# Placing attention's groups between projections by the planner's running estimate of TensorE's time

## Chip, cores and metric

The kernel runs on one core of a Trainium2 chip. The metric is the device time of one execution in microseconds (us); less is better. TensorE does the matmuls and transposes, VectorE, ScalarE and POOL (GpSimd) the elementwise work, and SyncE issues most of the DMAs from one queue (SPq in the rows).

## What is computed

One layer of a streaming encoder for 512 prompt tokens and 32 sample tokens (with 512 cached positions), width 1024, all in float32:

```python
h = rmsnorm(x, norm_mix); proj = h @ w_in            # q, k, v | RWKV-7 parts | gates A, B
o = diff_attend(q, k, v, lam, mask)                  # 8 heads, two softmax maps each
    # s = q k^T / 8 ; p = softmax(s) ; pd = p[0] - lam * p[1] ; o = pd @ v
o_da = (rmsnorm(o, da_subln) * (1 - lam_init)) @ w_o_da
o_rw = rwkv7_time_mixing(...) @ w_o_rw               # recurrence per token, group norm, gate
x = x + (sigmoid(gA) * o_da + sigmoid(gB) * o_rw) @ w_out
x = x + convffn(rmsnorm(x, norm_ffn)) ; y = rmsnorm(x, norm_final)
```

For the prompt the attention is causal by chunks of 64 tokens; for the sample it runs over the cache and its own 32 tokens, without a mask.

## The kernel before

**Stages.** The kernel computes the projections of `w_in` together with the recurrence, then attention, then the output projections (`w_orw`, `w_oda`, `w_out`) and the feed-forward part. The change lies in the attention stage, which begins when the recurrence's pools close (about 598 us in the profile) and ends when the first matmul of the `w_oda` projection starts (831 us).

**Projections.** `dense_g` (L229) makes one tile of 128 output columns. Weights and activations are split into high and low parts, so each of 8 steps of the inner dimension takes three matmuls of 128x128 by 272 columns, for each of two halves of the tokens: 16 steps a tile. A step ends at a `yield`. At the start of attention ten tiles of `w_in` are left (the gates; `fillers`, `fill_tile` L904), and eight tiles of the recurrence's output projection follow (`orw_g` L1392, which needs `z` from the recurrence in the split form `mh`, `ml`, loaded by `load_z` L1150, and a buffer `mg`).

**Attention.** `attention` (L1318) runs over 8 heads and four blocks of 128 queries each. One block is a series of groups of TensorE instructions: `scores` (L1283: four matmuls into `sc`, then maximum, exponential and the combination `pd` on VectorE and ScalarE); `weighted` (L1322: transposes of `pd`, a copy to `pdt` on ScalarE, products with V into `po`); after a head's last block `attend_norm` (L1137) and `finish_head` (L1346: transposes of `on`, stored as `dh`, `dl`). `weighted` of a block is traced after `scores` of the next one, across the end of a head too. The order of tracing for head h is: scores 0, transposes and products of block 3 of head h-1, scores 1, transposes and products 0, `finish_head` of h-1, scores 2, transposes and products 1, scores 3, transposes and products 2. `sc` has 3 buffers, `po` one.

**Loads.** `load_head` (L1256) is traced one head ahead. For Q and then for K it loads `raw` from memory, casts it to `hi` on ScalarE, subtracts on VectorE (in place, `lo = raw`) and writes both by DMAs to `Q`, `KH`, `KL` (two buffers each). `raw` and `hi` have one buffer each.

**Samples.** `samples` (L1377) makes attention for the 32 sample tokens in two groups of four heads (`attend_sample` L1183, five groups of TensorE instructions), the first after head 0, the second after head 2. Its cache lies in the buffer of `mg` (`load_caches` L1176), so `mg` can be used for the output projection only after the second group.

**What sets the order.** `Issue` (L62) keeps `PE.now`, an estimate of TensorE's time that every matmul and transpose advances by its own formula. `Flow.run` (L106) takes the next stream whose due time has come, and otherwise a step of the projections; without either it sets the clock forward. What comes out is the order of tracing, and this is the priority: the scheduler of the framework then goes through a model of the engines and gives each engine the earliest traced instruction whose inputs are ready there. In the kernel before, attention and samples run through `Flow.run` with due times that are always `PE.now` (L1324, L1334, L1347, L1356, L1364 and in `attend_sample` L1190, L1229, L1239, L1249) and with no projections (`Dense(lambda: None)`, L1383). So all of attention is traced first, all projections after it (L1385 on), and the scheduler pulls projections forward into TensorE's gaps. `keep_in_program_order` ties an instruction behind the one traced before it on its engine, in the order of issue only; before, `pinned` is never set.

Of the kernel before, what the change touches and what calls it, by code (L numbers as in the profile page):

```python
# [10 lines left out]
F32 = mybir.dt.float32  # L11
# [50 lines left out]
class Issue:  # L62
# [3 lines left out]
    def __init__(self, tc, pe):  # L66
        self.tc, self.pe, self.pinned, self.now, self.mode = tc, pe, False, 0.0, None

    def _add(self, ins, lhsT, rhs, out, passes):
        def n(x):  # L70
            return x.size() // x.shape[0] if callable(x.size) else x.size // x.shape[0]
        k, m, c = lhsT.shape[0], n(lhsT), n(rhs)
        mode = tuple(32 if v <= 32 else 64 if v <= 64 else 128 for v in (k, m))
        if passes == 1:
            t = c / 2400 + 0.0125
        else:
            t = passes * max(c / 1200, mode[1] / 1200) * (mode[0] / 128 if mode[1] < 128 else 1) * \
                (0.5 if mode[1] == 32 else 1)
        if mode != self.mode:
            t += 0.17  # L80
        self.mode = mode
        self.now += t
        if self.pinned:
            self.tc.keep_in_program_order(ins)
        return ins

# [75 lines left out]
def tile_hybrid_layer(  # L162
# [1020 lines left out]
    def attend_sample(g):  # L1183
# [5 lines left out]
        A.copy(out=vs, in_=ps[0:32].rearrange("p (e v) -> p e v", e=4))  # L1189
        yield PE.now  # L1190
        sc = [pssc.tile([128, 512], F32, name="sc", bufs=3) for _ in range(2)]
# [21 lines left out]
        for m in range(2):  # L1213
# [14 lines left out]
                               op0=ALU.mult, op1=ALU.add)  # L1228
        yield PE.now  # L1229
        ps = misc()  # L1230
# [7 lines left out]
        A.copy(out=pdtn, in_=ps[0:32, 0:128])  # L1238
        yield PE.now  # L1239
        po = misc().rearrange("p (a v) -> p a v", a=4)  # L1240
# [7 lines left out]
        on = attend_norm(po[:, 0:1, :], rz1[:, 0:1], 1)  # L1248
        yield PE.now  # L1249
        ps = misc()  # L1250
# [32 lines left out]
    def scores(i, Q, KH, KL, rz):  # L1283
# [32 lines left out]
        return pd  # L1316

    def attention():  # L1318
        prev = None
        last = {}  # L1320

        def weighted(h, i, pd, at, vtok, rz):  # L1322

            yield PE.now  # L1324
            ps = misc()
            for b in range(i + 1):
                PE.transpose(ps[:, b * 128:(b + 1) * 128], pd[:, b * 128:(b + 1) * 128], ident)
            pdt = ap.tile([128, 4, 128], F32, name="pdt", bufs=2)
            A.copy(out=pdt[:, 0:i + 1, :], in_=ps[:, 0:128 * (i + 1)].rearrange("p (b q) -> p b q", q=128))
            t = PE.now + 0.7 + 0.12 * i  # L1330
            if i == 0:
                t = max(t, po_free[0])
                last["po"] = None
            yield PE.now  # L1334
            if i == 0:
                last["po"] = pssc.tile([128, 4, 128], F32, name="po")
            po = last["po"]
            for b in range(i + 1):
                PE.matmul(po[:, i, :], pdt[:, b, :], vtok[:, b, :], start=(b == 0), stop=(b == i))
            if i == 3:  # L1340
                last["on"] = attend_norm(po, rz[:, :, 0], 4)
                last["at"] = PE.now + 5.5
                last["h"] = h
                po_free[0] = PE.now + 4.5

        def finish_head():  # L1346
            yield PE.now  # L1347
            ps = misc()
            on = last.pop("on")
            for i in range(4):  # L1350
                PE.transpose(ps[:, i * 128:(i + 1) * 128], on[:, i, :], ident)
            put_z(ps, last["h"], 0, SEQ)

        sc_free = 0.0
        nxt = load_head(0)
        yield PE.now  # L1356
        for h in range(HEADS):
            vt, Q, KH, KL = nxt
            if h + 1 < HEADS:
                nxt = load_head(h + 1)  # L1360
            vtok = tokens(vt)
            rz = ap.tile([128, 4, 2], F32, name="rz", bufs=2)
            for i in range(4):
                yield PE.now  # L1364
                pd = scores(i, Q, KH, KL, rz)
                sc_free = PE.now + 1.4 + 0.35 * (i + 1)
                ready = PE.now + 2.2 + 0.55 * (i + 1)
                if prev:
                    yield from weighted(*prev)
                if i == 1 and "on" in last:  # L1370
                    yield from finish_head()
                prev = h, i, pd, ready, vtok, rz
            flow.mark(("head", h))
        yield from weighted(*prev)
        yield from finish_head()

    def samples():  # L1377
        for g, h in ((0, 0), (1, 2)):
            load_caches(g)
            yield ("head", h), 0.0  # L1380
            yield from attend_sample(g)

    flow.run([samples(), attention()], Dense(lambda: None))  # L1383
    flow.mark("z", -1.0)
    for f in fillers:  # L1385
        for _ in f():
            pass
    zs = new_hl()
    mg = mp.tile([128, KT, TOK], F32, name="mg")
    load_z(mp, z_d, *zs, G)  # L1390

# [8 lines left out]

    for i in range(KT):
        for _ in orw_g(i):
            pass
    urgent[0] = False
# [286 lines left out]
```

## Time and profile before

| | |
|---|---|
| median of 3 runs | 1339.81 us (1338.94 to 1344.37) |
| profiled execution | 1342.24 us, span 1340.4 us |
| TensorE busy | 1241.1 us, 93% of the span |
| VectorE, ScalarE, POOL busy | 835.8, 592.1, 230.3 us |
| mean granted TensorE clock | 0.961 |
| attention stage | about 598 to 831 us of the span |

Busy times of TensorE include time in which a matmul's end is modelled, so a busy share says little about its speed; the granted clock (1.0 is 2.4 GHz, 0.5 is 1.2 GHz) and the count of matmuls in a stretch say more. Idle time matters only where the waiting engine is the one that ends last.

### The profile page before, as it was taken

The numbers are of one execution on the slowest core, as the hardware profiler recorded it, in microseconds if no ns is written. First come the engines' busy times: TensorE is split into PE (matmuls) and PEld (weight loads), VectorE is DVE, ScalarE is ACT, GpSimd is POOL, SyncE is SP. The second block draws the span as 40 slices with busy tenths as digits, with TensorE's granted clock in tenths as the row PEclk, the third lists the DMA queues.
The fourth block names the chain that finished last, engine by engine and source line by source line (L and its number), as shares of the span: only waits on it lengthen the run. The fifth ranks groups of instructions, "written<-read, shape, count | busy, mean of one in ns | idle before, by whom it ended". The sixth has DMA issues, their size and how long they took to land. (4 is left out here: it accounts for less than half of the span.)

```text
span 1340.4 us, 29785 instructions
## 1 busy us (share of the span) xinstructions
PE 1241.1 (93%) x12014; PEld 1181.3 (88%) x12014; DVE 835.8 (62%) x1721; ACT 592.1 (44%) x1192; POOL 230.3 (17%) x264
## 2 busy tenths in 40 slices
PE   8889997899868999999988986999999999999996
PEld 7889897788767998988776985999999999999996
DVE  6967769565873135650676664657877877773324
ACT  5656655565224333323665553334444444452220
POOL 6601122001221202223211100000111111111111
PEclk9899999799987999999998996999999999999998
DMA  5265554354772543538675550454222222243321
GB/s 173 81 191 166 186 166 150 97 159 133 237 232 67 169 149 121 173 107 274 202 227 170 168 155 25 129 174 141 87 95 88 87 88 88 87 136 116 107 75 67
DMA packets 140329, 185.75 MB, mean 139 GB/s; under 512 B 42016, under 2 KB 65184, under 8 KB 140192
## 3 DMA queue, kind: packets, MB, share of 16 engines
q1 hardware_dynamic: 127120, 162.60, 39.3%
q10 hardware_dynamic: 13072, 21.26, 4.7%
q8 instruction: 94, 1.54, 0.5%
q14 instruction: 43, 0.35, 0.1%
HBM read 133.54 MB, written 37.41 MB: 128 GB/s over the span
## 5 line engine op out<-in xcount | busy, mean ns | idle before, releaser
L225 ACT CAST wh<-wr 128x512 fp32r<-128x512 f32 (+1 forms) x316 | 193.4, 614 | 344.2 <-PE psd L88 300.5
L88 PE MATMUL psd<-h_h,wh 128*128 128x272 f32 x976 | 293.7, 301 | 9.0 <-ACT qt L909 4.7
L88 PE MATMUL psd<-h_h,wl 128*128 128x272 f32 x976 | 288.7, 296 | 0.0
L88 PE MATMUL psd<-h_l,wh 128*128 128x272 f32 x976 | 287.2, 294 | 0.0
L226 DVE TENSOR_TENSOR wl<-wr,wh 128x512 fp32r<-128x512 f32 x230 | 157.7, 688 | 126.4 <-ACT wh L225 115.9
L88 PE MATMUL psd<-xgh,wl 128*128 128x272 f32 x704 | 204.0, 290 | 0.0
L88 PE MATMUL psd<-xgh,wh 128*128 128x272 f32 x704 | 203.0, 288 | 0.0
L88 PE MATMUL psd<-xgl,wh 128*128 128x272 f32 x704 | 202.2, 287 | 0.0
L88 PEld LDWEIGHTS psd<-h_h,wh 128*128 128x128 f32 x976 | 188.5, 193 | 15.5 <-ACT qt L909 5.8
L88 PEld LDWEIGHTS psd<-h_h,wl 128*128 128x128 f32 x976 | 188.4, 193 | 4.9 <-issue 3.6
L88 PEld LDWEIGHTS psd<-h_l,wh 128*128 128x128 f32 x976 | 188.6, 193 | 3.0 <-issue 2.3
L226 POOL TENSOR_TENSOR wl<-wr,wh 128x512 fp32r<-128x512 f32 x86 | 118.1, 1375 | 390.3 <-ACT wh L225 348.3
L88 PEld LDWEIGHTS psd<-xgl,wh 128*128 128x128 f32 x704 | 132.7, 189 | 0.0
L88 PEld LDWEIGHTS psd<-xgh,wl 128*128 128x128 f32 x704 | 132.3, 188 | 0.0
L88 PEld LDWEIGHTS psd<-xgh,wh 128*128 128x128 f32 x704 | 132.2, 188 | 0.1
L88 PE MATMUL psd<-ah,wh 128*128 128x272 f32 x352 | 101.7, 289 | 0.0
L88 PE MATMUL psd<-ah,wl 128*128 128x272 f32 x352 | 101.5, 288 | 0.0
L88 PE MATMUL psd<-al,wh 128*128 128x272 f32 x352 | 101.4, 288 | 0.0
L1489 POOL COPY cvo<-uf 128x2 f32<-128x2 f32 x88 | 37.3, 454 | 219.8 <-DVE uf L1486 219.8
L88 PE MATMUL psd<-ml,wh 128*128 128x272 f32 x256 | 74.9, 293 | 0.0
L88 PE MATMUL psd<-mh,wl 128*128 128x272 f32 x256 | 74.7, 292 | 0.0
L88 PE MATMUL psd<-mh,wh 128*128 128x272 f32 x256 | 74.4, 291 | 0.0
(373 smaller groups left out, 2531.9 us busy)
## 6 DMA issues: line engine op xcount, KB each, us to landing
wr<-w_in SPq DMA_DIRECT2D x132, 256.0 KB, 3.2
wr<-w_up SPq DMA_DIRECT2D x88, 256.0 KB, 2.7
wr<-w_down SPq DMA_DIRECT2D x40, 256.0 KB, 2.6
bkL<-bk_d SPq DMA_DIRECT2D x16, 512.0 KB, 4.2
ar_d<-ar SPq DMA_DIRECT2D x8, 544.0 KB, 4.0
t_d<-qt ACTq DMA_DIRECT2D x16, 272.0 KB, 2.4
bk_d<-bk SPq DMA_DIRECT2D x32, 128.0 KB, 3.4
arL<-ar_d SPq DMA_DIRECT2D x8, 512.0 KB, 4.1
```

Source lines behind the costliest of these rows:

```text
L88: ins = self.pe.matmul(out, lhsT, rhs, **kw)
L225: A.copy(out=wh[:, :n], in_=raw)
L226: le.tensor_tensor(out=wl[:, :n], in0=raw, in1=wh[:, :n].bitcast(F32), op=ALU.subtract)
L1489: G.tensor_copy(out=cvo[:, t, :, w], in_=u[:, 512 + w::32])
```

## The change

- `PE.hold`, set before a group, ties the first TensorE instruction of that group (and only this one) behind the TensorE instruction traced before it.
- Due times are now real: each group of attention and samples is traced only when `PE.now` has passed an estimate of when its inputs are ready (score buffers free 2.6 + 0.9 per block after the scores, products 1.4 + 0.12 i after the transposes, the norm's transposes 7.5 after the products, and so on); the first head starts 14 after the stage's start.
- `Flow.run` gets the projections: while no group is due, a step of the fillers is traced, and then of the output projection, as soon as `z` is marked as loaded and the second sample group is done. What is left of them comes after attention.
- `load_z` is traced after head 1 instead of after the fillers; its tiles `mh`, `ml` are taken before `mg`.

No instruction on any engine is added or dropped.

```diff
@@ class Issue
-        self.tc, self.pe, self.pinned, self.now, self.mode = tc, pe, False, 0.0, None
+        self.tc, self.pe, self.hold, self.now, self.mode = tc, pe, False, 0.0, None
...
-        if self.pinned:
+        if self.hold:
             self.tc.keep_in_program_order(ins)
+            self.hold = False
@@ attend_sample
-        yield PE.now
+        yield PE.now + 1.5
+        PE.hold = True
         sc = [pssc.tile([128, 512], F32, name="sc", bufs=3) for _ in range(2)]
...
-        yield PE.now
+        yield PE.now + 6.5
+        PE.hold = True
...
-        yield PE.now
+        yield PE.now + 2.0
+        PE.hold = True
         po = misc().rearrange("p (a v) -> p a v", a=4)
...
-        yield PE.now
+        yield PE.now + 7.0
+        PE.hold = True
@@ attention
+    zs = new_hl()
+
     def attention():
...
         def weighted(h, i, pd, at, vtok, rz):
 
-            yield PE.now
+            yield at
+            PE.hold = True
...
-            t = PE.now + 0.7 + 0.12 * i
+            t = PE.now + 1.4 + 0.12 * i
             if i == 0:
                 t = max(t, po_free[0])
                 last["po"] = None
-            yield PE.now
+            yield t
+            PE.hold = True
...
             if i == 3:
                 last["on"] = attend_norm(po, rz[:, :, 0], 4)
-                last["at"] = PE.now + 5.5
+                last["at"] = PE.now + 7.5
                 last["h"] = h
                 po_free[0] = PE.now + 4.5
 
         def finish_head():
-            yield PE.now
+            yield last["at"]
+            PE.hold = True
...
         nxt = load_head(0)
-        yield PE.now
+        yield PE.now + 14.0
...
             for i in range(4):
-                yield PE.now
+                yield sc_free
+                PE.hold = True
                 pd = scores(i, Q, KH, KL, rz)
-                sc_free = PE.now + 1.4 + 0.35 * (i + 1)
-                ready = PE.now + 2.2 + 0.55 * (i + 1)
+                sc_free = PE.now + 2.6 + 0.9 * (i + 1)
+                ready = PE.now + 3.0 + 0.6 * (i + 1)
...
             flow.mark(("head", h))
+            if h == 1:
+                load_z(mp, z_d, *zs, G)
+                flow.mark("z", 30.0)
@@ after samples
             yield from attend_sample(g)
-
-    flow.run([samples(), attention()], Dense(lambda: None))
-    flow.mark("z", -1.0)
-    for f in fillers:
-        for _ in f():
-            pass
-    zs = new_hl()
-    mg = mp.tile([128, KT, TOK], F32, name="mg")
-    load_z(mp, z_d, *zs, G)
+            flow.mark(("sample", g))
...
-    for i in range(KT):
-        for _ in orw_g(i):
-            pass
+    under = list(range(KT))
+    mg = None
+
+    def choose2():
+        nonlocal mg
+        if fillers:
+            return fillers.pop(0)()
+        if not under or "z" not in flow.done or ("sample", 1) not in flow.done:
+            return None
+        if mg is None:
+            mg = mp.tile([128, KT, TOK], F32, name="mg")
+        return orw_g(under.pop(0)) if flow.done["z"] <= PE.now else None
+
+    att_dense = Dense(choose2)
+    flow.run([samples(), attention()], att_dense)
+    att_dense.finish()
+    while att_dense.step():
+        att_dense.finish()
     urgent[0] = False
```

## Rows read from the trace of the kernel before

**Rows 1.** Stretches of heads 6 and 7: from:to, length, busy (count) per engine, clock.

```profile
781.35:804.65 23.30, 19.36 (x132) 18.18 (x132) 15.29 (x48) 11.84 (x36) 0.00 (x0) 0.89 0.64 167
804.65:831.10 26.45, 13.56 (x56) 11.08 (x56) 12.99 (x51) 9.62 (x37) 0.00 (x0) 0.63 0.10 28
```

**Rows 2.** Projection matmuls (`psd`) on TensorE between heads' first scores: from:to, length, busy (count), clock.

```profile
598.50:631.85 33.35, 30.12 (x234) 1.00 0.85 264
631.85:657.50 25.65, 15.89 (x109) 1.00 0.67 195
657.50:685.10 27.60, 16.67 (x116) 1.00 0.79 251
685.10:709.10 24.00, 10.79 (x71) 1.00 0.62 178
709.10:737.30 28.20, 11.50 (x72) 0.82 0.63 181
737.30:759.35 22.05, 13.13 (x89) 1.00 0.55 163
759.35:781.35 22.00, 14.79 (x102) 1.00 0.56 155
781.35:804.65 23.30, 10.62 (x73) 0.89 0.64 167
804.65:831.10 26.45, 0.00 (x0) 0.63 0.10 28
```

**Rows 3.** Timeline of SyncE's queue, last K issue of heads 0, 4, 6, 7.

```profile
631.90 1.24 SPq L1272 DMA_DIRECT2D KL<-raw  x2
...
737.12 1.25 SPq L1272 DMA_DIRECT2D KL<-raw  x2
...
781.69 1.25 SPq L1272 DMA_DIRECT2D KL<-raw  x2
...
803.03 1.25 SPq L1272 DMA_DIRECT2D KL<-raw  x2
```

**Rows 4.** Timeline of TensorE from 800 us: start, length, line, out<-in, [idle before].

```profile
801.16 1.06 PE L92 MATMUL tp<-cst,pd 128*128 128x128 f32 x4
802.95 2.08 PE L88 MATMUL po<-vtok,pdt 128*128 128x128 f32 x8 [0.73 <-ACT pdt L1329]
804.68 1.09 PE L88 MATMUL sc<-KH,Q 128*128 128x256 f32 x3
...
811.27 0.69 PE L88 MATMUL sc<-KH,Q 128*128 128x384 f32 x1 [4.25 <-ACT E L1308]
...
814.36 0.78 PE L88 MATMUL sc<-KH,Q 128*128 128x512 f32 x1
...
820.31 1.65 PE L88 MATMUL po<-vtok,pdt 128*128 128x128 f32 x6 [0.63 <-ACT pdt L1329]
...
823.55 2.08 PE L88 MATMUL po<-vtok,pdt 128*128 128x128 f32 x8 [0.73 <-ACT pdt L1329]
830.41 1.09 PE L92 MATMUL tp<-cst,on 128*128 128x128 f32 x4 [4.79 <-DVE on L1146]
831.15 0.58 PE L88 MATMUL psd<-dh,wh 128*128 128x272 f32 x1
```

**Rows 5.** Chain that ended last, the piece before head 7's K.

```profile
791.28 4.05 DMA Q<-raw
...
795.39 2.91 DMA raw<-k_d
...
798.67 0.62 ACT hi L1266
```

**Rows 6.** Waits of TensorE, 598 to 797 us: first and last of eight.

```profile
PE tp L92 <- DVE on L1146: 3.2, 2, 1.8
...
PE sc L88 <- DMA KH<-hi: 1.0, 2, 0.8
```

**Rows 7.** Waits of SyncE's queue, 600 to 832 us: the one for `mg`.

```profile
SPq L1393 <- PE tp L88: 4.8, 1, 4.8
```

## Prediction

> **What bounds the kernel now.** I read the page's slices first: TensorE is busy nearly everywhere, except in a few stretches, and the attention stage (from about 598 us to 831 us) is the one that the diff touches. So I read that stage by stretches, from one head's first scores to the next [rows 1]. In the second row, the last head, no projection is left: TensorE is busy 13.56 of 26.45 us at a mean granted clock of 0.63, a mixture of its two levels (1.2 and 2.4 GHz). In the first it is busy 19.36 of 23.30 us. TensorE is not what is short here.
>
> Next, where the projections lie. [rows 2] counts their matmuls between the first scores of successive heads. Three make one step of the generator; 864 in all are 288 steps or 18 tiles (10 fillers and 8 of the recurrence's output projection; the rows add up to 866, two from the tile before). They are all done before the last head begins, although the stage ends 26 us later. More room on TensorE would only end them sooner.
>
> What then paces the heads? [rows 3] shows the queue's issue of the last low parts of K, one row for the first head and the fifth, seventh and eighth. Each head's first scores start with them: head 7's K is issued from 803.03 us and its scores start at 804.68 us [rows 3, 4]. Between heads 6 and 7 lie 21.34 us, between heads 0 and 7 171.1 us, or 24.4 each. `load_head` has one `raw` and one `hi` buffer, so Q, then K, then the next head's Q go through them one by one. The chain of waits runs through just this: Q's low part 4.05 us, K's load 2.91 us, K's cast 0.62 us [rows 5]. So **a chain of loads paces the heads**, at about 21.3 us where nothing disturbs it; seven periods at that rate are 149.4 us, and 21.7 us went to queues that were busy with something else. After the last load comes a tail from 804.68 to 831.15 us [rows 4], 26.5 us, which is pure latency: scores, maximum, exponentials, transposes, products, norm.
>
> **The change part by part.** Nothing is removed or added on any engine: every matmul, copy and DMA stays. Three things move.
>
> *Lower bounds.* Before, all of attention is traced ahead of all projections, and the scheduler may pull any group forward. After, the first instruction of each group is tied behind the TensorE instruction traced before it. Where that lies follows from the planner's arithmetic. A dense step counts 3 x (272/2400 + 0.0125) = 0.378 us. For a steady head the path of due times is: first scores 0.48, transposes 0.44, copy 1.76, products 0.85, norm 7.5, its transposes 0.44, third scores 0.69, wait 5.3, fourth scores 0.90, wait 6.2; in all 24.6 us, and about 0.6 us because a due time is met only at the end of a step: 25.2 us. Attention's own counted time is 6.7 us of it, which leaves 18.5 us or 49 steps of projections in each head. With the start of 14 us (37 steps), the small groups of the samples, and no step available from the end of the fillers (160) until the second sample is done, the first scores of heads 0 to 7 stand behind 37, 80, 122, 160, 173, 222, 271 and 288 steps. The trace of before has done 78, 114, 153, 177, 201, 230, 264 and 289 by then (running sums of [rows 2] over 3). So **the bounds are slack by 41 to 8 steps up to head 5**, because the real first scores wait for loads that the planner does not know of. Only head 6 is short, by 7 steps or 2.6 us; its remaining groups have room for that (below). I cost the bounds at 0; if that cover goes, see the slower rival.
>
> *Order among the groups.* The tie also works between attention's groups, and here it binds at every head. Before, the transposes and products of head h-1's last block go ahead of head h's scores, which still wait for K: products at 802.95 us, scores at 804.68 us [rows 4]. Afterwards they are tied behind those scores, and the third scores of the head are tied behind the transposes of the norm that follow from those products. From the scores X of the last head, by durations of [rows 4]: the first four of the eight score matmuls 1.2 us; transposes to products 802.95 - 801.16 = 1.8 us; products to the norm's transposes 830.41 - 823.55 = 6.9 us; the transposes 1.1 us. That puts the third scores at X + 11.0, against 811.27 - 804.68 = 6.6 before: **4.4 us later**. From there to the end the same work remains (831.15 - 811.27 = 19.9 us). Bounds: +4.4 if it takes as long, 0 if VectorE, which then has the first two blocks' work behind it, makes the delay good; I take +4, near the end that is read from rows. In the earlier heads the same delay is there but covered by the load chain: by the same rows, X + 11.0, + 3.1 to the fourth scores, + 6.0 to the third block's products and 1.7 for them is X + 21.8, all with durations of the half-clocked tail; at full clock half of the 4.0 us of matmuls in it (1.2, 1.1 and 1.7) goes and it is about 20, under the 21.3 of the loads. It is a thin cover, and the rival below is what happens if it tears.
>
> *The z load, the samples and `mg`.* The loads of z are traced after head 1 instead of last, but the scheduler already let them run in gaps; 8 copies on ScalarE and 8 subtractions on POOL move by little and nothing waits for them: 0. The second sample's groups are now interleaved with head 3's. Its products free the buffer of `mg`; the queue waits 4.8 us for that [rows 7], with the Q load of head 4 right behind it. If the sample ends later by the groups now ahead of it (two score groups and head 2's last block, each a wait of 1 to 2 us), the load chain slips by up to 5 us; if the scheduler then issues the Q load first, it gains 2.8 us. The trace of before can't show which; between -2.8 and +5 I take +1, nearer the middle because the chain's later waits absorb part of either.
>
> *TensorE's waits.* While there are projections TensorE waits 16.6 us in eight groups of waits, of 3.2 down to 1.0 us [rows 6]. Waits for order replace some of them. Worth 0 on the time: the projections end before the last load anyway.
>
> **Sum.** 0 + 4 + 1 + 0 = +5. The profiled execution took 1342.24 us (span 1340.4 and 1.8 around it), so 1347.2 on its base; it lies 2.4 us over the median of the three runs, 1339.81, and against that median I forecast **1345 us**.
>
> **The rivals.** *Slower: order tears the loads' cover.* If in the filled stretch the strict chain of groups takes more than 21.3 us a head (VectorE is busy 15.29 of 23.30 us there, 12.99 of 26.45 in the tail [rows 1], so every step of it queues longer), the heads run at the planner's own period. Three periods follow after head 4; in [rows 3] they took 65.9 us from 737.12 to 803.03, at 25.2 they take 75.6: +9.7. With the tail's +4 that is 1354 us. For it: the margin is only about 1.5 us. Against: the bounds themselves are slack. It decides from the point where a head's fourth scores come later than about 15 us after its first.
>
> *Faster: the load chain is relieved.* 21.7 us of the 171.1 are not the chain's own. They are casts and subtractions that stand in ScalarE's and VectorE's queues behind attention's instructions that wait for TensorE. If groups that come in order and spread out leave these queues freer, half of it, 10.9, comes back; with the tail's +4 and the queue's -2.8 that is 1330 us. For it: the lost time lies in heads 0 to 4, where the samples crowd in. Against: nothing in the diff gives the loads a buffer or a place.
>
> *Faster: TensorE's gaps are the price.* If every wait of [rows 6] vanished and the stage ended as much earlier, the time would be 1339.8 - 16.6 = 1323 us. The Trainium skill, Perfetto Trace Analysis, section Optimization Strategies, says that the goal is in general to keep the matmul engine at high utilization, and that one should go after whatever blocks it when it idles. By that rule this is the outcome; the rows speak against it, since the projections end before the last head begins [rows 2].
>
> *No change.* If the scheduler, whose bounds are mostly slack, comes to the same order, it is 1340 us.
>
> **How the numbers follow.** Forecast 0.38, slower rival 0.24, relieved loads 0.22, gaps 0.08, no change 0.08. What a measurement here can tell from no change is about 0.5%, 6.7 us: under 1333.1 is faster, over 1346.5 slower. The forecast's own spread (its terms' bounds together: -2.8 to +9.4) leaves 0.27 inside and 0.11 above. Relieved loads: 0.16 faster, 0.06 inside; gaps 0.08 faster; slower rival 0.22 above, 0.02 inside; no change inside. Faster 0.24, same 0.43, slower 0.33. Range: the gaps' 1323 and the lower part of the relieved loads are left out below (0.12), the upper third of the slower rival above (0.08): 1328 to 1357.
>
> **What would show it.** Right: the distances between the last K issues stay at 21 to 23 us in the last three heads; head 7's third scores come about 11 us after its first; the norm's transposes stand ahead of them; projections end some 5 to 40 us before the stage. Wrong: a last head with projections beside it and no long tail (the bounds did bind, and usefully); K issues 24 us or more apart in heads 5 to 7 (slower rival); or the sum of the first four distances, now 105.2 us [rows 3], falling by several us (relieved loads). A stage that ends at the same time with other positions would show that neither order nor bounds matter.

## The result

The changed kernel is a little slower. The two were timed side by side:

| | before | after |
|---|---|---|
| median of 8 runs | 1345.41 us (1338.94 to 1354.52) | 1352.96 us (1349.24 to 1355.65) |
| ratio | | 1.0058, 95% interval 1.0033 to 1.0084 |
| profiled execution (span) | 1342.24 us (1340.4) | 1353.59 us (1351.8) |
| TensorE busy, mean granted clock | 1241.1 us, 0.961 | 1243.1 us, 0.954 |
| first cache load of the stage to first matmul of `w_oda` | 603.96 to 831.15, 227.2 us | 605.28 to 841.60, 236.3 us |
| head 0's last K issue to first matmul of `w_oda` | 631.90 to 831.15, 199.2 us | 634.87 to 841.60, 206.7 us |

The forecast was 1345 us for a kernel before of 1339.81, or 0.4% slower; measured is 0.6% slower. Of the 8.0 us between 1345 and 1352.96, 5.6 are the kernel before itself (1345.41 over eight runs where the first three gave 1339.81); the change's own part is 7.6 us where 5 were foreseen. The sum is nearly right, its terms are not.

From the first matmul of `w_oda` to the end of the span both take about the same (509.3 and 510.2 us). So the difference lies in the attention stage. Of the 9.1 us by which it grew, 1.6 lie ahead of head 0's last K issue (27.9 and 29.6 us from the first cache load). That stretch takes 27.9 to 30.0 us in all the kernels here with one `raw` buffer, so this part is not put down to the change. After, line numbers are one to five higher than before up to `scores` (`scores` L1313 for L1308, loads L1277 for L1272).

The last three stretches, as in [rows 1]: from:to, length, then busy us (count) of TensorE, weight loads, VectorE, ScalarE and POOL, then granted clock, DMA share and GB/s.

```profile
768.85:795.35 26.50, 25.76 (x203) 25.09 (x202) 17.53 (x50) 13.35 (x38) 3.84 (x3) 1.00 0.61 170
795.35:812.95 17.60, 13.47 (x101) 12.51 (x101) 13.05 (x44) 10.33 (x33) 0.00 (x0) 0.98 0.47 135
812.95:841.50 28.55, 14.88 (x73) 12.41 (x72) 14.17 (x53) 10.96 (x40) 0.00 (x0) 0.74 0.06 20
```

The first is head 5: TensorE is busy 25.76 of 26.50 us. In this head it has become what is short. The last is the tail without projections, 2.1 us longer than before.

Projections between the first scores of successive heads, as in [rows 2]:

```profile
598.50:635.20 36.70, 32.59 (x243) 0.95 0.80 243
635.20:660.20 25.00, 15.93 (x109) 1.00 0.71 211
660.20:688.90 28.70, 18.31 (x128) 1.00 0.81 247
688.90:714.90 26.00, 8.54 (x59) 0.87 0.61 169
714.90:738.05 23.15, 0.00 (x0) 0.69 0.54 143
738.05:768.85 30.80, 19.38 (x138) 0.90 0.59 174
768.85:795.35 26.50, 20.46 (x149) 1.00 0.61 170
795.35:812.95 17.60, 7.35 (x53) 0.98 0.47 135
812.95:841.50 28.55, 0.00 (x0) 0.74 0.06 20
```

The fifth row has none at all: below, "the hole" is the time in which no projection runs. A matmul across a boundary is counted in both rows. Counted once, by their starts on TensorE's timeline, and over 3, 78, 114, 156, 176, 176, 222, 271 and 288 steps stand ahead of the first scores of heads 0 to 7. The planner's positions are 37, 80, 122, 160, 173, 222, 271 and 288. Up to head 3 there is room, and head 4 has 3 steps of it. For heads 5 and 6 the two numbers are the same. That is how a lower bound looks that binds. For head 7 it no longer does by itself: the last projection starts 8.9 us ahead of its first scores, and only attention's groups of head 6 lie between.

```profile
804.06 0.29 PE L89 MATMUL psd<-mh,wl 128*128 128x272 f32 x1
```

The queue's last K issues of heads 0, 4, 6 and 7, as in [rows 3]:

```profile
634.87 1.23 SPq L1277 DMA_DIRECT2D KL<-raw  x2
...
731.59 1.24 SPq L1277 DMA_DIRECT2D KL<-raw  x2
...
782.03 1.24 SPq L1277 DMA_DIRECT2D KL<-raw  x2
...
802.58 1.25 SPq L1277 DMA_DIRECT2D KL<-raw  x2
```

Head 7's K comes 167.7 us after head 0's (171.1 before): the loads are earlier than they were. But the scores no longer start with them. TensorE's timeline of the tail, as in [rows 4]:

```profile
812.99 0.56 PE L89 MATMUL sc<-KH,Q 128*128 128x256 f32 x1
...
823.04 0.76 PE L89 MATMUL po<-vtok,pdt 128*128 128x128 f32 x2 [4.34 <-DVE on L1147]
823.60 1.06 PE L93 MATMUL tp<-cst,on 128*128 128x128 f32 x4
824.31 0.67 PE L89 MATMUL sc<-KH,Q 128*128 128x384 f32 x1
...
840.86 1.09 PE L93 MATMUL tp<-cst,on 128*128 128x128 f32 x4 [4.79 <-DVE on L1147]
841.60 0.58 PE L89 MATMUL psd<-dh,wh 128*128 128x272 f32 x1
```

Head 7's first scores start at 812.99, 10.4 us after the K issue at 802.58 (1.65 us before). The third scores follow 11.3 us later, behind the norm's transposes of head 6.

TensorE's waits from 598 to 842 us, the largest in total (us, times, longest; those of before, up to 797 us, are in [rows 6]):

```profile
PE po L89 <- DVE on L1147: 15.5, 7, 4.3
```

It has grown from 1.7 us before: products of a head's first block, which need the only `po` buffer, stand in a fixed place and wait there for the norm of the head before. The queue's wait for `mg` [rows 7] has shrunk from 4.8 to 0.3 us.

**Where the hole comes from.** Five moments of before: the second sample's first scores, the last projection ahead of the hole, the sample's products, the load of `mg` right behind them, and the first projection after the hole.

```profile
700.26 1.04 PE L88 MATMUL sc<-mg,qks 64*32 64x512 f32 x2
...
708.70 0.28 PE L88 MATMUL psd<-mh,wl 128*128 128x272 f32 x1
...
714.74 1.94 PE L88 MATMUL tp<-mg,pdt 128*32 128x128 f32 x32
...
716.74 0.33 SPq L1393 DMA_DIRECT2D mg<-t_d  x1
...
720.10 0.39 PE L88 MATMUL psd<-mh,wh 128*128 128x272 f32 x1
```

The same in the changed kernel, from the last projection ahead of the hole to the first behind it:

```profile
699.02 0.29 PE L89 MATMUL psd<-mh,wl 128*128 128x272 f32 x1
...
713.85 1.09 PE L89 MATMUL sc<-mg,qks 64*32 64x512 f32 x16
...
727.61 0.80 PE L89 MATMUL po<-vtok,pdt 128*128 128x128 f32 x2 [3.25 <-DVE on L1147]
728.34 1.94 PE L89 MATMUL tp<-mg,pdt 128*32 128x128 f32 x32
...
732.93 1.49 SPq L1399 DMA_DIRECT2D mg<-t_d  x3
...
741.92 0.75 DVE L1319 SCALAR_TENSOR_TENSOR pd<-E,Z 128x512 f32<-128x512 f32 x1
742.58 0.78 DVE L1403 SCALAR_TENSOR_TENSOR mg<-mg,psd 128x272 f32<-128x272 f32 x2
...
744.02 0.37 PE L89 MATMUL psd<-mh,wh 128*128 128x272 f32 x1
```

After 176 steps the first tile of the output projection is done but can't leave its PSUM buffers, since its evacuation needs `mg`, and `mg` is free only after the second sample's products. In the fixed order these stand behind head 2's last blocks, head 3's scores and products that wait for a norm, and come 13.6 us later than before (10.6 counted from head 0's last K issue). The projections stand still for 45 us (11 before).

The sample's lateness is not all of it. Counted from head 0's last K issue the hole begins 12.7 us sooner than before and ends 21.0 later. From the sample's products to the next projection are 15.7 us (5.4 before): the load of `mg` is issued behind the writes of head 4's K and lands 3.1 us later, at 736.0, but the evacuation follows only at 742.58, right behind the `pd` of head 3's last block. VectorE sat idle from 736.14 to 737.53 in between. That reads as a wait for its place in VectorE's order, behind attention's work, and not for `mg`.

### The profile page after: what moved, and what is told of

Same layout as the page of the kernel before. It is cut to its first block, busy times and chain, and to the rows that moved or that the text cites. A ratio compares the mean times of both kernels' runs of the same rounds, so it can differ in the third digit from the quotient of the medians.

```text
span 1351.8 us, 29764 instructions
## 1 busy us (share of the span) xinstructions
PE 1243.1 (92%) x12014; PEld 1186.9 (88%) x12014; DVE 838.1 (62%) x1721; ACT 592.6 (44%) x1192; POOL 231.4 (17%) x264
## 4 chain that ended last, share of the span: by engine, by line
PE 68%; DVE 9%; DMA 3%; ACT 3%; issue 2%; SPq 1%; POOL 0%; DVEq 0%; ACTq 0%
PE psd L89 53%; PE misc L89 4%; PE psq L89 3%; PE psy L89 2%; PE misc L93 2%; PE sc L89 2%; PE po L89 2%; PE tp L93 2%; DVE wl L227 1%; DMA t_d<-qt 0%; DMA kout<-cs 0%; SPq L1277 0%; DMA raw<-k_d 0%; DVE on L1147 0%; DMA raw<-q_d 0%
```

## The experiments

The theory at this point: the strict order makes the second sample late, the hole grows, and the bounds then hold heads 5 and 6, and through them head 7, behind projections that the hole has delayed. The rival: the order among the groups alone costs it. In all that follows the stage is counted from its first cache load to the first matmul of `w_oda` (227.2 us before, 236.3 after). Ratios are of medians, to the kernel before timed beside that run; positions and stage lengths are read from one execution each, and can be off by several us.

**Order without projections between.**

```diff
-    flow.run([samples(), attention()], att_dense)
+    flow.run([samples(), attention()], Dense(lambda: None))
+    flow.mark("z", -1.0)
```

> The changed kernel, with its due times, its order among attention's and the samples' groups and its ties, but with all projections traced behind attention as in the kernel before: no group stands behind a projection any more, the only lower bounds left are those between groups. Theory (bounds): the loss of the changed kernel (1.0058 of before) lies in bounds that put heads 4 to 7 behind projections that the hole at 700 to 743 us had delayed. Then here head 7's first scores come back to 803 to 807 us (after: 812.99, before: 804.68), only the tail's +2 us (28.6 against 26.5 us) stays, and the ratio to before is 1.000 to 1.003. The hole itself stays, since the second sample's groups are still in strict order. Rival (order among groups): strict order alone costs it; then the ratio is 1.005 to 1.008 and head 7 starts at 811 us or later with no projection held ahead of it.

Measured: 1.0000 (0.9976 to 1.0024), 1346.54 us against 1346.73; stage 230.5 us. TensorE's tail:

```profile
804.82 0.36 PE L89 MATMUL sc<-KH,Q 128*128 128x256 f32 x1
...
816.61 0.67 PE L89 MATMUL sc<-KH,Q 128*128 128x384 f32 x1
...
834.93 1.09 PE L93 MATMUL tp<-cst,on 128*128 128x128 f32 x4 [4.79 <-DVE on L1147]
835.67 0.57 PE L89 MATMUL psd<-dh,wh 128*128 128x272 f32 x1
```

Head 7 starts with its loads again, 171.0 us after head 0's last K issue (172.8 before, 178.1 in the changed kernel). So against the kernel before, the order among groups alone does not make head 7 late; with the bounds behind projections it is late. Two things temper this. The hole is shorter here too (703.03 to 729.58 us, 26.6). And the last three distances between K issues are 26.0, 23.2 and 22.7 us, together 6.0 more than before; the first four, together 6.7 less, make up for it. The tail is 30.9 us, 4.4 more than before: third scores 11.8 us after the first (6.6 before). Here I had expected only 2. In this execution this part of the order costs what the prediction gave it. The ratio does not show a loss; its interval reaches to 3.2 us.

**The same order of tracing without ties.**

```diff
-        if self.hold:
+        if False:
             self.tc.keep_in_program_order(ins)
```

> The changed kernel with its order of tracing but without any tie: each group keeps its priority only. Theory (bounds): nothing is held, so the first scores follow the loads again, head 7 at 803 to 806 us, tail 26 to 27 us, second sample's scores back near 700 us, ratio 0.997 to 1.002. Rival (the new order of tracing, as priority, is the cause): the projections that are now traced ahead of later groups win against them without any tie, heads 5 to 7 start late (head 7 at 810 us or more) and the ratio stays at 1.004 to 1.007.

Measured: 0.9951 (0.9928 to 0.9974), 1338.94 us, better than the theory had it; stage 223.3 us. Head 7's last K issue comes 164.9 us after head 0's and its scores begin with it; the end lies 28.4 us behind that issue (28.1 before).

```profile
724.41 1.08 PE L89 MATMUL tp<-mg,pdt 128*32 128x128 f32 x32
...
799.81 0.55 PE L89 MATMUL sc<-KH,Q 128*128 128x256 f32 x1
...
800.57 1.23 SPq L1277 DMA_DIRECT2D KL<-raw  x2
```

The second sample's first scores are back at 700.94 us; its products are only partly, 88.8 us after head 0's last K issue (82.8 before, 93.5 in the changed kernel), and the hole is 19.7 us, behind a gap of 7.0. So neither due times nor tracing order as a mere priority cost anything. The ties make the difference of 1.0058 to 0.9951.

Two things go beyond the theory. The steps ahead of heads 5 and 6 are 222 and 271 here as well, though nothing ties them; but they are done in time, so head 5 starts with its K issue and head 6 4.3 us behind it (7.2 and 13.4 in the changed kernel). And of the 1.1% between no ties and the changed kernel, only 0.6 is the step from order alone (1.0000) to the changed kernel (1.0058). The other 0.5 lies between no ties and order alone, two kernels timed beside each other: in order alone head 7's K issue comes 170.4 instead of 164.9 us after head 0's. They differ in the projections' priority as well, so how much of this is the order among groups is not shown.

**The second sample after head 1.**

```diff
-        for g, h in ((0, 0), (1, 2)):
+        for g, h in ((0, 0), (1, 1)):
```

> The changed kernel with the second sample after head 1 instead of head 2, so that it is done before the fillers end. By the planner's arithmetic the first scores of heads 3 to 7 then stand behind 160, 209, 258, 288 and 288 steps. Theory (hole and bounds): the hole at 700 to 743 us closes, the projections run through and are done at about 785 us; the bounds of heads 4 and 5 bind by little, head 6 starts at 782 to 788 and head 7 at 803 to 809 us, a head of 20 to 21 us later; with the longer tail the ratio to before is 0.998 to 1.003, 4 to 8 us better than the changed kernel. Rival (order among groups costs it): head 7 starts at 811 us or later although there is no hole, ratio 1.005 or more.

Measured: 0.9952 (0.9930 to 0.9974), 1340.90 us; stage 223.2 us. Projections from head 3 to head 6:

```profile
682.78:703.82 21.04, 11.98 (x83) 1.00 0.77 230
703.82:728.58 24.76, 14.95 (x106) 1.00 0.64 178
728.58:753.09 24.51, 17.86 (x125) 1.00 0.65 172
753.09:772.87 19.78, 12.80 (x88) 1.00 0.63 171
772.87:793.97 21.10, 0.00 (x0) 0.70 0.56 140
```

There is no hole (no gap over 5 us), and with all ties in place head 7 starts at 793.97 us, 166.1 us after head 0's last K issue. By the planner's arithmetic the bounds are even higher here (209, 258 and 288 steps ahead of heads 4 to 6), and they cost little (first scores 0.0 to 3.3 us behind the K issues of heads 4 to 7) once the projections run through: this one line takes 1% from the changed kernel. It is the hole and the bounds together.

**The output projection released 22 us of planner's time later.**

```diff
-            flow.mark(("sample", g))
+            flow.mark(("sample", g), 22.0)
...
-        if not under or "z" not in flow.done or ("sample", 1) not in flow.done:
+        if not under or "z" not in flow.done or flow.done.get(("sample", 1), 1e9) > PE.now:
```

> The changed kernel with the output projection released 22 us of the planner's time after the second sample, everything else the same: by the planner's arithmetic the first scores of heads 4 to 7 stand behind 160, 173, 222 and 271 steps, one head later than in the changed kernel (173, 222, 271, 288). Theory (bounds): the hole stays as long as it is, but no bound reaches into it; heads 5 to 7 follow the loads, head 7 starts at 803 to 808 us, the last 17 steps (about 6 us) lie beside head 7's waits, ratio to before 0.997 to 1.002. Rival (order among groups): unchanged, 1.004 to 1.008. Rival (the hole itself costs it by the work that it defers): projections end later, in the tail, and the ratio is 1.004 or more with a head 7 that starts in time.

Measured: 1.0031 (1.0007 to 1.0055), 1351.62 us; stage 234.7 us. Projections in two stretches:

```profile
716.42:744.38 27.96, 0.00 (x0) 0.66 0.42 109
...
808.49:842.13 33.64, 5.46 (x34) 0.73 0.20 57
```

The bounds let go of heads 5 to 7: head 7 starts at 808.49 us with its K issue (808.66), 172.9 us after head 0's, as before. But the gain went elsewhere. Against the changed kernel, head 7's scores come 10.5 us less behind their loads, the loads 5.4 us later (173.1 us from head 0's last K issue to head 7's) and the tail is 5.0 us longer: nothing is left. Head 4 starts in the hole, where the granted clock is 0.66, 108.8 us after head 0's last K issue (103.2 in the changed kernel); whether this is what delays the loads was not tried. The tail, with 34 projection matmuls between its groups, takes 33.6 us, 7 more than before. The expected 0.997 to 1.002 was missed. What came is the picture of the last rival, a head 7 in time and projections in the tail; its 1.004 lies within the interval. That bounds bind behind the hole was right, that moving them would be free was not.

**Two buffers for `raw` in the kernel before.** Was it right that a chain of loads paced it?

```diff
-            raw = ap.tile([128, SEQ], F32R, name="raw")
+            raw = ap.tile([128, SEQ], F32R, name="raw", bufs=2)
...
-        En = ap.tile([128, 2, 32], F32, name="En")
+        En = spare[g][:, 128:192].rearrange("p (a t) -> p a t", a=2)
-        pdtn = ap.tile([32, 128], F32, name="pdtn")
+        pdtn = spare[g][0:32, 0:128]
```

`spare[g]` is the unused end of the cache's buffer, `c[:, 8 * PAST:8 * PAST + 256]`; without this the second buffer doesn't fit.

> The kernel before with two buffers for raw (and, to make room, the samples' small tiles pdtn and En in the unused end of the cache's buffer): a load no longer waits for the writes of the one before. Theory (a chain of loads paces the heads of the kernel before): each of the two loads of a head loses about 3.4 us of waiting for raw, the distance between last K issues falls from 21 to 27 us to 15 to 20 us, limited then by attention's own chain and by TensorE, which still has all its projections; the last K issue of head 7 comes 140 to 160 us after head 0's (171.1 before), projections lie beside the last heads, ratio 0.985 to 0.994. Rival (the loads are not what paces, TensorE or the chain of groups is): K issues come earlier but first scores stay where they are, or K issues don't move, ratio 0.998 to 1.002.

Measured: 0.9884 (0.9852 to 0.9916), 1330.07 us; stage 210.5 us. The last head, columns as in [rows 1]:

```profile
764.05:813.16 49.11, 47.27 (x369) 45.59 (x368) 28.59 (x90) 22.00 (x66) 7.85 (x6) 1.00 0.26 79
```

Head 7's K comes 137.8 us after head 0's (171.1 before, 140 to 160 expected). Projections now fill the tail, which TensorE ends at full clock, busy 47.27 of 49.11 us. The load chain was the pace, as read from [rows 3] and [rows 5].

**The same two buffers in the changed kernel.** Edit as above.

> The changed kernel with the same two buffers for raw. Theory (bounds): heads 4 to 7 wait for projections, not for loads, so earlier loads bring little: first scores of head 7 stay behind 288 steps, ratio to the kernel before 1.001 to 1.006, at most 5 us better than the changed kernel, and the last K issue lies 10 us or more ahead of the first scores in heads 5 to 7. Rival (loads pace here too): the same gain as the kernel before has from the two buffers, 8 us or more.

Measured: 0.9989 (0.9967 to 1.0011), 1343.71 us; stage 224.0 us. From 1.0058 that is some 9 us: more than the 5 us I had allowed, and less than the 15.4 us that the kernel before gained, so the ratio missed the theory's range, and of the rival only its bound of 8 us was met, not "the same gain". Head 7's K and first scores:

```profile
790.49 1.24 SPq L1278 DMA_DIRECT2D KL<-raw  x2
...
804.62 0.48 PE L89 MATMUL sc<-KH,Q 128*128 128x256 f32 x1
```

The scores stand 14.1 us behind the loads (19.7 and 21.6 in heads 5 and 6, behind 222 and 271 steps), so the bounds bind as before and part of the buffer's worth is lost. The hole is shorter: earlier heads bring the second sample's products to 721.16 us (728.34), and the projections stand still from 715.7 to 730.9 us, 15 instead of 45 us. That this is where the 9 us come from is likely, but was not tried by itself.

**Early sample without ties.** Both edits from above in one kernel.

> The changed kernel with the second sample after head 1 and without ties. If the longer tail (32.3 us from the last K issue to the end of attention with ties and the early sample, 28.1 us before, 28.4 us without ties) is the price of the order among groups, it falls back to 28 to 29 us here, while the heads keep the earlier loads of the run with the early sample (last K issue of head 7 162.8 us after head 0's): 191 us from head 0's last K issue to the end of attention (before 199.2, changed kernel 206.7, early sample 195.1, no ties 193.4), ratio 0.990 to 0.994. Rival (the ties are what brought the gain of the run with the early sample, by keeping an order that frees the loads): 195 us or more, ratio 0.995 or more.

Measured: 0.9966 (0.9945 to 0.9987), 1342.26 us; stage 224.7 us. The tail from the last K issue is 29.2 us (32.3 with ties), as expected if the order costs 3 to 4 us there. But the rest came as the rival had it (195 us or more, 0.995 or more): head 7's K comes 167.2 us after head 0's (162.8 with ties), and 196.4 us lie between head 0's issue and the end instead of 191. The loss lies between heads 2 and 3 (29.4 us against 23.5); which instruction stood in the loads' way there I did not find. The intervals of the three runs (no ties, early sample, both) overlap, so no order among them is claimed: with the early sample the ties cost nothing that shows.

**Early sample and two buffers, with ties.**

> The changed kernel with the second sample after head 1 and two buffers for raw, with ties. Theory: with the hole closed and the loads faster, the heads are paced by the planner's bounds, whose period is 25.2 us of its clock while projections last (23.3 us on the chip in the run with the early sample alone); little comes on top of 0.9952: 0.992 to 0.996. Rival (loads still pace the heads once the hole is closed): the gain of the two buffers comes in full, 0.985 to 0.991.

Measured: 0.9967 (0.9945 to 0.9989), 1340.51 us; stage 224.7 us. The loads are early (158.1 us from head 0's to head 7's last K issue), yet head 7's first scores come at 801.9 us, 15 us behind theirs. The ratio lies just above the 0.992 to 0.996 of the theory, far from the rival's. The heads stand behind the planner's steps (161, 210, 259 and 288 ahead of heads 3 to 6, by its arithmetic 160, 209, 258 and 288): 23.8, 24.6, 24.4, 30.3, 28.2 us from one to the next as long as projections last. Behind them, the chain of groups takes 19.3 and 21.9 us. With the ties and the hole closed, faster loads are worth nothing (0.9952 without them); with the hole they had brought 9 us.

**Early sample in the kernel before.** One line, as above.

> The kernel before (no due times, no ties) with the second sample after head 1. Theory (the loads pace the kernel before, the hole matters only together with bounds): the hole of 12 us closes, but projections were not what ended last; what comes back is at most the queue's wait of 4.8 us for the cache buffer, which now lies at another head: ratio 0.996 to 1.001. Rival (the hole itself is worth what the early sample brought to the changed kernel, from 1.0058 to 0.9952): 0.990 to 0.994.

Measured: 0.9962 (0.9943 to 0.9981), 1340.41 us, the lower end of what was expected; stage 221.5 us. In the kernel before the hole is worth some 5 us, in the changed kernel 14 (1.0058 to 0.9952), and in the changed kernel without ties nothing that shows (0.9951 and 0.9966).

**Early sample and two buffers in the kernel before.**

> The kernel before with two buffers for raw and the second sample after head 1. With two raw buffers alone TensorE is full only from the last head's first scores on (47.3 of 49.1 us) and lacks projections for 8, 14, 5 and 5 us at 703 to 779 us, as the output projection waits for the second sample and its loads. Theory (with faster loads the projections end last, so the hole now counts): the early sample fills 10 to 20 us of it, ratio 0.974 to 0.984. Rival (TensorE's clock or the loads take it back): 0.986 to 0.990, as with two raw buffers alone.

Measured: 0.9899 (0.9867 to 0.9931), 1331.36 us; stage 219.4 us. Nothing was added to 0.9884: the rival holds. (The two profiled executions differ by 8.9 us in the stage, the medians by 1.3: an example of how far one execution can be off.) The output projection still stood still, now for `z`: its eighth part was split at 749.84 us, since `load_z` comes last in priority in the kernel before.

**The same with `load_z` after head 1**, which is the one part of the change that this needs:

```diff
+    zs = new_hl()
     def attention():
...
             flow.mark(("head", h))
+            if h == 1:
+                load_z(mp, z_d, *zs, G)
...
-    zs = new_hl()
     mg = mp.tile([128, KT, TOK], F32, name="mg")
-    load_z(mp, z_d, *zs, G)
```

> The kernel before with two buffers for raw, the second sample after head 1 and the loads of z traced after head 1 as in the changed kernel. In the run without the last part the output projection still stood still from 694 to 750 us, since the last of the eight parts of z was split at 749.8 us (VectorE's and the cache buffer no longer held it). Theory: z comes by about 690 to 700 us, the projections run through, TensorE is full to the end of the stage, which ends 10 to 18 us earlier than with two raw buffers alone; ratio 0.976 to 0.984. Rival (attention's order is then what suffers, since the z work takes ScalarE's and the queue's time from the loads): 0.986 to 0.992.

Measured: 0.9839 (0.9816 to 0.9862), 1324.91 us, the best of all and ahead of both kernels; stage 208.8 us. The ratio lies at the upper end of the theory's range, but against two `raw` buffers alone the stage is only 1.8 us shorter in the profiled executions, and 0.45% (6 us) by the ratios, where 10 to 18 were expected. Its last head:

```profile
769.26:814.15 44.89, 43.45 (x336) 41.82 (x337) 25.57 (x78) 19.43 (x55) 6.48 (x5) 1.00 0.28 84
```

The eighth part of `z` comes at 691 us, and TensorE is busy 43.45 of 44.89 us at the end. From 674 to 719 us there are still gaps in the projections of 9 and 5 us, and of 6 and 9 us around the second sample at 643 to 661 us.

**`load_z` right after the first head's loads instead.**

> The same with the loads of z traced right after the first head's loads. Theory: z is there at about 650 us, the rest as in the run before, ratio 0.974 to 0.984, with the first two heads up to 3 us later. Rival: the z work in the first heads delays the load chain by more than it gives, 0.986 to 0.992.

Measured: 0.9862 (0.9841 to 0.9884), 1329.16 us; stage 212.5 us. Heads 0 and 1 lie 25.7 us apart by the very last issue of their K (16.2 in the run before): the `z` work goes ahead of the loads (`z` is there at 672 us, 650 expected), and the rival holds.

## Why the prediction came out nearly right, for reasons partly wrong

Counted from head 0's last K issue the stage grew by 7.5 us. The timelines split that into three: the loads, -3.4 (171.1 to 167.7 us); head 7's scores behind their loads, +8.8 (1.65 to 10.4 us); the tail from there, +2.1 (26.5 to 28.6 us). The forecast had +1, 0 and +4 there. That its sum of 5 comes near 7.5 is luck: the term put at 0 came to 8.8, and loads and tail that came out 4.4 and 1.9 better than forecast make up for most of it.

- **What bounds the kernel before: right.** Two buffers for `raw` in it take 1.2% off, and its tail then fills with projections. "More room on TensorE would only end them sooner" holds nearly: closing the hole alone brought 0.4%, and the last projection then started 180.0 instead of 191.3 us after the stage's first cache load.
- **Lower bounds, costed at 0: wrong, and the step that failed.** Head 7's scores came 8.8 us later behind their loads, held through heads 5 and 6. The planner's positions were worked out rightly. The slack, 41 to 8 steps, was counted against the steps that the kernel *before* had done by each head. The change itself delays those steps, so the cover was taken from the wrong kernel: 222 steps ahead of head 5, just its bound, where 230 stood.
- **The samples and `mg`, +1: mis-sized and half seen.** The second sample's delay was foreseen ("two score groups and head 2's last block"), but followed only into the load queue, where I feared up to 5 us. There the wait for `mg` nearly disappeared instead, and the distance from head 3 to head 4 fell from 27.1 to 19.8 us. That the same delay stops the projections, whose evacuation needs the same buffer, was not followed at all, nor was the 6.5 us that the evacuation then waited on VectorE. This is where the prediction lost its cover.
- **Order among groups, +4: right in mechanism, +2.1 in the changed kernel.** Third scores at X + 11.3 (X + 11.0 foreseen); from there to the end 17.3 instead of 19.9 us, the part "VectorE makes good". In the kernel with the order alone it was +4.4. That the order stays covered in earlier heads holds there for head 7's start against the kernel before, but the last three K distances, 26.0, 23.2 and 22.7 us, are over the 21.3 of the loads: how thin the cover is stays open.
- **TensorE's waits, 0: not shown, and its reason fell.** Waits of 15.5 us for the norm came (1.7 before). "The projections end before the last load" no longer holds: the last one starts at 804.06, the last K issue is at 802.58 us. From head 4's first scores to head 7's TensorE waits 6.1 us, in heads that no longer wait for loads; what they cost was not tried by itself.
- **The slower rival** had the right sum for three periods, by luck, and mostly the wrong cause. From head 4's first scores to head 7's lie 74.9 us; it said 75.6, from the planner's 25.2 us a head. But the single periods are 30.8, 26.5 and 17.6 us. It wanted a chain of groups longer than the loads; from head 6 to head 7, where only 17 steps of projections were left, it takes 17.6 us, and the two long periods come from bounds behind projections.
- **The relieved loads** came in part: 3.4 us in the changed kernel, 6.2 without ties and 8.3 with the early sample, where the rival had put 10.9. Its sign came more clearly: the first four distances fell from 105.2 to 96.7 us in the changed kernel. The last three rose from 65.9 to 71.0 (30.1, 20.3 and 20.6, where 21 to 23 each were foreseen), and the bounds kept the rest from being used.
- **TensorE's gaps** (1323 us): the gaps stayed, and projections were not what ended last. The Trainium skill, Perfetto Trace Analysis, section Optimization Strategies, asks for a matmul engine that is kept busy. The combined kernel agrees with it (TensorE busy 43.45 of 44.89 us at its end, 1324.91 us), but got there by a load buffer, an earlier sample and an earlier `z`, not by pacing.

**Not settled:** why the loads come earlier in these three kernels. The wait for `mg`, 4.8 us before [rows 7], can be no more than a part of it: the stretch from head 3 to head 4 fell by 7.3 us in the changed kernel, fell to 22.8 us without ties although the queue still waits 3.5 us for `mg` there, and stayed at 26.5 us in the kernel before with the early sample, where that wait is gone.

## What to carry to other kernels

A lower bound on an instruction costs what the work ahead of it is late, so count the slack in the order that the change will make, not in the trace of before, and follow each delayed step to every user of the buffer that it frees. A planner that knows only one engine can set priorities, as here without ties, but when it fixes places it passes each delay that it doesn't know of (a load, a buffer) on to everything behind. Where a chain through one staging buffer paces the work, a second buffer (here 2 kB a partition) was worth more than any order tried alone (1.2% against 0.5%).

## What the runs showed of the chip

The place of the stage in the span varies more than the change's effect: its first cache load lies between 598.07 and 608.74 us in executions of kernels whose code is the same up to there. Stages have to be compared by their lengths.

A hole in the projections slows attention as well. In the changed kernel the granted clock falls to 0.69 from 714.90 to 738.05 us, where TensorE has only attention's groups, a mixture of 2.4 and 1.2 GHz; eight products of one block take 2.08 us there and 1.16 us once projections run again (TensorE's timeline at 720.25 and 745.00 us):

```profile
720.25 2.08 PE L89 MATMUL po<-vtok,pdt 128*128 128x128 f32 x8 [1.62 <-ACT pdt L1337]
...
745.00 1.16 PE L89 MATMUL po<-vtok,pdt 128*128 128x128 f32 x8
```
